# Decoding chosen expert pairs through two one-hot rows of 16, and giving all weight splits of routing to GpSimd

## The chip, the cores and the metric

The kernel runs on one core of one Trainium2 chip. The metric is the device time of one execution in microseconds; the median of the runs is given. In the profile PE is TensorE, DVE VectorE, ACT ScalarE, POOL GpSimd and SP SyncE, which issues the loads.

## The reference

Two layers of a network for 512 tokens with 1024 features. The first is a layer with sparse attention and a state-space branch; the second has a band attention, a gated delta rule and, at its end, `peer`, in which the change lies. `peer` takes 128 tokens at a time:

```python
qry = rms_norm_2((hb @ w_query).reshape(128, 8, 256), query_gain)
s1 = einsum("thd,nd->thn", qry[..., :128], sub_keys_1)      # 128 keys
s2 = einsum("thd,nd->thn", qry[..., 128:], sub_keys_2)      # 128 keys
v1, i1 = top_k(s1, 16)
v2, i2 = top_k(s2, 16)
cand_s = (v1[..., :, None] + v2[..., None, :])              # 16 x 16 pairs
cand_i = (i1[..., :, None] * 128 + i2[..., None, :])
top_s, pos = top_k(cand_s, 16)
experts = take_along_axis(cand_i, pos, axis=-1)
gates = softmax(top_s)
u, vv = expert_down[experts], expert_up[experts]
act = gelu(einsum("thkd,td->thk", u, hb))
out = einsum("thk,thkd->td", gates * act, vv)
```

So each token and each of 8 heads picks 16 of 16384 experts: for each chosen pair the position among the candidates has to be turned into the two key numbers.

## The kernel before, in words

Instructions are recorded in Python order and a scheduler then sets a fixed order for each engine; an engine works through its own queue in that order and waits at its head. A matrix product is done with operands split in two parts, high and low, in three passes (`mm3`, L71 to L74). Weights are loaded by SP into `wr`, ScalarE makes the high part `wh` (L51), and `wl`, the low part, is a subtraction on VectorE or GpSimd (L52), 128 x 1024 elements; the parameter `eng` says which.

`peer` has these stages. `routing` makes the 16 query projections and then, for token blocks 3, 0, 1, 2 of 128 tokens, the choice of experts. Tokens of blocks 0, 1 and 2 go through all experts densely: `down` is one projection of 384 tokens on 128 experts with a GELU, `g_build` makes the weights of the experts, `up_block` and `up_mm` multiply by the second matrix. Tokens of block 3 take their experts' rows by indirect DMA, issued on GpSimd (`gather_steps`), and multiply them on VectorE (L1667, L1680). `fill(x, eng)` puts x `down` projections at the place where it is called, as work for TensorE; its `eng` goes to the split of the weights. `gstep(n)` puts n gather steps there.

In `routing`, `best(t)` makes the scores of two heads at a time on TensorE (L1405), ScalarE copies them to `sc` (L1406), and VectorE finds the 16 best of 128 keys with MAX8, FIND_INDEX8 and MATCH_REPLACE8 (L1410 to L1414). `choose(t)` then forms 50 candidate sums `cand` for each of 8 heads (of 16 x 16 pairs only those with (a + 1)(b + 1) up to 16 can be chosen), finds the 16 best and their positions `pf`, and decodes the positions. `code` holds 128 i1 + i2 of the 50 candidates, built on GpSimd in `codef`. For two heads at a time VectorE compares `pf` with `iota50` into `eq` (L1459), 50 rows of 16, GpSimd multiplies `eq` by `code` as 32-bit words (L1463), and six additions on VectorE sum the 50 rows (L1465), cast to `ex` (L1466). `route_end` makes the softmax of the 16 sums; for block 3 it casts `ex` to `idx`, the gather's list; for the others it takes `ex` apart into the two keys by a shift and a mask (L1511 to L1517), transposes them on TensorE and leaves 16-bit lists for `g_build`.

`choose` of one block and `best` of the next are generators that alternate: after each `yield` of `choose`, `best` does two heads. Block 3's `best` runs alone first.

Of the kernel before, what the change touches and what calls it, by code (L numbers as in the profile page):

```python
# [20 lines left out]
P = 128  # L21
# [5 lines left out]
class Kernel:  # L27
# [1318 lines left out]
    def routing(self, rt):  # L1346
        nc, I, pp, pr = self.nc, self.i, self.pp, self.pr
        V, G = nc.vector, nc.gpsimd
# [3 lines left out]
        for j in range(2):  # L1352
            k = self.load(rt, f"peer_k{j}", [P, P])
            V.tensor_scalar(k, k, qg[:, j:j + 1], None, op0=OP.mult)
            keys.append(k)
        iota50 = self.t(rt, [P, 50, 16], F16, "iota50")
        G.iota(iota50, [[1, 50], [0, 16]], base=0, channel_multiplier=0, allow_small_or_imprecise_dtypes=True)
        sel = self.t(rt, [P, 8, 8], F32, "sel")
        G.affine_select(sel, self.ones[:, :64].rearrange("p (a b) -> p a b", a=8), [[1, 8], [-1, 8]],
                        OP.is_equal, 0.0, base=0, channel_multiplier=0)  # L1360
# [15 lines left out]
        p = self.t(pr, [P, T], F32, "a", 5)  # L1376
# [16 lines left out]
        def best(t, out):  # L1393

            tt = slice(t * P, t * P + P)
            vv = self.t(rt, [P, 8, 2, 16], F32, "vv", 2)
            ii = self.t(rt, [P, 8, 2, 16], U32, "ii", 2)
            out += [vv, ii]
            for hp in range(4):
                ps = self.t(pr, [P, T], F32, "a", 5).rearrange("p (a n) -> p a n", a=4)  # L1400
                s = self.t(rt, [P, 4, P], F32, "sc", 2)
                for j in range(2):
                    h = 2 * hp + j
                    for k in range(2):
# [12 lines left out]
                self.fill(1.25, G if hp % 2 else None)  # L1417
                yield

        def choose(t, vv, ii):  # L1420

            fi = self.t(rt, [P, 8, 2, 16], F32, "fi", 1)
            V.tensor_copy(fi, ii)
            V.tensor_scalar(fi[:, :, 0], fi[:, :, 0], 128.0, None, op0=OP.mult)

            cand = self.t(rt, [P, 8, 50], F32, "cand", 1)
            code = self.t(rt, [P, 8, 50], I32, "code", 1)
            codef = self.t(rt, [P, 8, 50], F32, "codef", 1)
            off = 0
            for a in range(9):  # L1430
                n = 16 // (a + 1) if a < 8 else 8
                o = slice(off, off + n)
                for eng, dst, src in ((V, cand, vv), (G, codef, fi)):
                    if a < 8:
                        eng.tensor_add(dst[:, :, o], src[:, :, 1, :n], src[:, :, 0, a:a + 1].to_broadcast([P, 8, n]))  # L1435
                    else:
                        eng.tensor_add(dst[:, :, o], src[:, :, 0, 8:16], src[:, :, 1, 0:1].to_broadcast([P, 8, n]))
# [12 lines left out]
            pf = self.t(rt, [P, 8, 16], F16, "pf", 1)  # L1450
            V.tensor_copy(pf, pi_)
            yield
            ex = self.t(rt, [P, 8, 16], F32, "ex", 1)
            for h in range(0, 8, 2):

                sh = [P, 2, 50, 16]
                hh = slice(h, h + 2)
                eq = self.t(rt, sh, I16, "eq", 3)
                V.tensor_tensor(eq, pf[:, hh].unsqueeze(2).to_broadcast(sh), iota50[:, None].to_broadcast(sh),  # L1459
                                op=OP.is_equal)  # L1460

                e2 = eq.bitcast(I32)
                G.tensor_mul(e2, e2, code[:, hh].unsqueeze(3).to_broadcast([P, 2, 50, 8]))  # L1463
                for m, n in ((25, 25), (13, 12), (7, 6), (4, 3), (2, 2), (1, 1)):
                    self.pace = V.tensor_tensor(eq[:, :, :n], eq[:, :, :n], eq[:, :, m:m + n], op=OP.add)  # L1465
                V.tensor_copy(ex[:, hh], eq[:, :, 0])  # L1466
                if t != 3:
                    self.gstep(1)
                self.fill(1, G)
                if h == 2:  # L1470
                    yield
            self.fill(2, G)
            self.route_end(rt, t, ts, ex)
# [16 lines left out]

    def route_end(self, rt, t, ts, ex):

        nc, pp, pr = self.nc, self.pp, self.pr
        V = nc.vector
        sh = [P, 8, 16]
        e = self.t(rt, sh, F32, "ge", 1)
        V.tensor_sub(e, ts, ts[:, :, 0:1].to_broadcast(sh))
        nc.scalar.activation(e, e, AF.Exp)
        sm = self.t(rt, [P, 8], F32, "gs", 1)
        V.tensor_reduce(sm, e, axis=AX.X, op=OP.add)  # L1500
        V.reciprocal(sm, sm)
        fl = "p h k -> p (h k)"
        if t == 3:
# [280 lines left out]
```

## Time and profile before

| | us |
|---|---|
| median of 3 runs | 2604.02 |
| lowest and highest run | 2603.02, 2606.86 |
| the profiled execution | 2602.06 |
| its span, first to last instruction | 2600.3 |
| TensorE, VectorE, ScalarE, GpSimd busy | 2458.6, 1889.7, 1052.5, 709.0 |

Busy time is the time in which an engine had at least one instruction running. In the rows below, a line number is a line of the kernel before; `out<-in` are tiles by the program's names; after a bar come busy time and the mean duration of one, then the idle time of the engine just ahead of those instructions and what ended it.

### The profile page before, as it was taken

Reading aid. Unit: us, or ns where it says so; the run is one execution under the profiler, and the core shown is the slowest. Engines: PE = TensorE matmul, PEld = TensorE weight load, DVE = VectorE, ACT = ScalarE, POOL = GpSimd, SP = SyncE. Lnnn points to the kernel's source line nnn. Section 1 sums busy time; section 2 is a strip of 40 time slices with the busy share of each in tenths; the row PEclk is TensorE's granted clock in tenths of the full one; section 3 lists DMA queues with packets and bytes.
Section 4 is the critical chain, followed back from the end, with each engine's and each line's share of the span. In section 5 each row is a group of like instructions: output and inputs, shape, how many; then the busy total and the mean of one; then the engine's idle time right before and its main releaser. Section 6 shows DMA issues by size and latency. Waiting matters only on the chain. (4 is left out here: it accounts for less than half of the span.)

```text
span 2600.3 us, 34898 instructions
## 1 busy us (share of the span) xinstructions
PE 2458.6 (95%) x12577; PEld 2051.7 (79%) x12577; DVE 1889.7 (73%) x3704; ACT 1052.5 (40%) x1881; POOL 709.0 (27%) x554
## 2 busy tenths in 40 slices
PE   5999999999999999899998887999989999999999
PEld 4777777768788779776778887899978888888887
DVE  8795666667764773565428899998767788888877
ACT  4444466653322444344433333354433333333332
POOL 3240011010001122511104566321344343443431
PEclk9999999999999999999999988999999999999999
DMA  7222212228865311111322455698999999989995
GB/s 243 77 81 83 72 65 65 74 75 298 283 225 172 98 57 49 49 37 57 128 81 82 149 175 160 230 328 319 338 333 319 336 337 343 352 305 334 341 333 211
DMA packets 199597, 500.44 MB, mean 192 GB/s; under 512 B 20096, under 2 KB 85888, under 8 KB 196352
## 3 DMA queue, kind: packets, MB, share of 16 engines
q1 hardware_dynamic: 159104, 338.81, 39.2%
q0 software_dynamic: 36864, 134.23, 14.6%
q10 hardware_dynamic: 3456, 25.17, 2.4%
q8 instruction: 99, 1.62, 0.3%
q14 instruction: 74, 0.61, 0.1%
HBM read 448.01 MB, written 50.14 MB: 192 GB/s over the span
## 5 line engine op out<-in xcount | busy, mean ns | idle before, releaser
L74 PE MATMUL g<-hh,wl 128*128 128x384 f32 (+1 forms) x1792 | 663.6, 370 | 42.0 <-DVE wl L52 23.2
L51 ACT ACTIVATE wh<-wr 128x1024 fp32r<-128x1024 f32 (+2 forms) x424 | 442.7, 1046 | 630.8 <-PE g L73 345.8
L72 PE MATMUL g<-hh,wh 128*128 128x384 f32 (+1 forms) x1792 | 668.3, 373 | 9.4 <-ACT act L1624 7.8
L73 PE MATMUL g<-hl,wh 128*128 128x384 f32 (+1 forms) x1792 | 660.4, 369 | 0.0
L52 DVE TENSOR_TENSOR wl<-wr,wh 128x1024 fp32r<-128x1024 f32 (+3 forms) x370 | 453.7, 1227 | 210.8 <-ACT wh L51 208.6
L74 PEld LDWEIGHTS g<-hh,wl 128*128 128x128 f32 x1792 | 344.5, 192 | 81.2 <-DVE wl L52 24.8
L72 PEld LDWEIGHTS g<-hh,wh 128*128 128x128 f32 x1792 | 344.5, 192 | 44.3 <-ACT act L1624 8.7
L73 PEld LDWEIGHTS g<-hl,wh 128*128 128x128 f32 x1792 | 344.1, 192 | 40.6 <-issue 10.3
L73 PE MATMUL acc<-wl,gh 128*128 128x512 f32 x768 | 303.8, 396 | 0.0
L74 PE MATMUL acc<-wh,gl 128*128 128x512 f32 x768 | 303.7, 395 | 0.0
L72 PE MATMUL acc<-wh,gh 128*128 128x512 f32 x768 | 303.7, 395 | 0.0
L1661 POOL DMA_INDIRECT row<-in_rows_dn,idx x128 | 162.9, 1273 | 342.2 <-DVE row L1667 289.9
L1661 POOL DMA_INDIRECT row<-in_rows_up,idx x128 | 173.1, 1352 | 271.5 <-DVE gacc L1680 250.8
L51 ACT ACTIVATE gh<-ga 128x384 fp32r<-128x384 f32 x128 | 67.2, 525 | 336.1 <-issue 196.4
L52 POOL TENSOR_TENSOR wl<-wr,wh 128x1024 fp32r<-128x1024 f32 x54 | 132.7, 2463 | 214.0 <-ACT wh L51 204.2
L1667 DVE SCALAR_TENSOR_TENSOR row<-row,h2n 128x1024 f32<-128x1024 f32 x128 | 160.6, 1261 | 23.1 <-DMA row<-in_rows_dn,idx 23.0
L1680 DVE SCALAR_TENSOR_TENSOR gacc<-row,gw,gacc 128x1024 f32<-128x1024 f32 x127 | 162.5, 1280 | 12.9 <-DMA row<-in_rows_up,idx 12.2
L74 PEld LDWEIGHTS acc<-wh,gl 128*128 128x128 f32 x768 | 144.4, 188 | 34.7
L73 PEld LDWEIGHTS acc<-wl,gh 128*128 128x128 f32 x768 | 144.4, 188 | 34.4
L72 PEld LDWEIGHTS acc<-wh,gh 128*128 128x128 f32 x768 | 144.4, 188 | 34.4
L52 DVE TENSOR_TENSOR gl<-ga,gh 128x384 fp32r<-128x384 f32 x128 | 73.2, 572 | 58.0 <-ACT gh L51 58.0
L98 PE MATMUL g<-wh,hh 128*128 128x512 f32 (+3 forms) x256 | 96.1, 377 | 13.4 <-ACT hh L223 11.8
(551 smaller groups left out, 3919.8 us busy)
## 6 DMA issues: line engine op xcount, KB each, us to landing
wr<-in_w_dn SPq DMA_DIRECT2D x128, 512.0 KB, 4.7
wr<-in_w_up SPq DMA_DIRECT2D x128, 512.0 KB, 6.8
wr<-in_ada_w SPq DMA_DIRECT2D x56, 512.0 KB, 4.6
g_d<-stage ACTq DMA_DIRECT2D x24, 1024.0 KB, 9.0
gr<-g_d SPq DMA_DIRECT2D x32, 768.0 KB, 9.6
wr<-in_w_x SPq DMA_DIRECT2D x24, 512.0 KB, 3.4
act_d<-act SPq DMA_DIRECT2D x63, 192.0 KB, 4.8
ar<-act_d SPq DMA_DIRECT2D x63, 192.0 KB, 6.1
```

The source lines that it names most:

```text
L51: nc.scalar.activation(hi, src, AF.Copy)
L52: eng.tensor_sub(lo, src, hi.bitcast(F32))
L72: mm(ps, ah, bh, start=first, stop=False)
L73: mm(ps, ah, bl, start=False, stop=False)
L74: self.mm = mm(ps, al, bh, start=False, stop=last)
L98: mm(pss[t], hh[:, tt], wh[:, k], start=f, stop=False)
L1661: nc.gpsimd.indirect_dma_start(r, None, src, bass.IndirectOffsetOnAxis(ap=self.idx[:, s:s + 1], axis=0))
L1667: nc.vector.scalar_tensor_tensor(r, r, 1.0, self.h2n, op0=OP.mult, op1=OP.mult, accum_out=act[:, s:s + 1])
L1680: nc.vector.scalar_tensor_tensor(acc, r, w[:, s:s + 1], acc, op0=OP.mult, op1=OP.add)
```

## The change

The position of a chosen candidate is no longer looked up in a list of 50 codes. The candidates lie in rows: row a of the first eight has 16 // (a + 1) entries, so a comparison with the start of each next row (`first`) counts the row number, and a product with the row lengths (`count`) sums up where the row starts. That gives, for each of 128 chosen positions, the two ranks a and b below 16. The last 8 positions are the ranks 8 to 15 of the first key with rank 0 of the second, added by `px`. Then one comparison with `iota16` makes one-hot rows of 16 for all heads and both keys, 4096 f16 elements; they are multiplied by the key numbers `iif` and summed in four halvings to the two keys `f1`. All of it is on VectorE. `codef`, `code`, the multiplication on GpSimd, and the taking apart in `route_end` go; for block 3, 128 times the first key plus the second is formed in `route_end`. The fills of routing all give GpSimd as the engine of their splits, two of them at another place in `choose`; the gather steps stand in pairs.

```diff
-        iota50 = self.t(rt, [P, 50, 16], F16, "iota50")
-        G.iota(iota50, [[1, 50], [0, 16]], base=0, channel_multiplier=0, allow_small_or_imprecise_dtypes=True)
+        iota16 = self.t(rt, [P, 16, 16], F16, "iota16")
+        G.iota(iota16, [[1, 16], [0, 16]], base=0, channel_multiplier=0, allow_small_or_imprecise_dtypes=True)
+        first = self.t(rt, [P, 8, P], F16, "first")
+        count = self.t(rt, [P, 8, P], F16, "count")
...
+            G.memset(first[:, j], float(off))
+            G.memset(count[:, j], float(n))
...
-                self.fill(1.25, G if hp % 2 else None)
+                self.fill(1.25, G)
...
-            fi = self.t(rt, [P, 8, 2, 16], F32, "fi", 1)
-            V.tensor_copy(fi, ii)
-            V.tensor_scalar(fi[:, :, 0], fi[:, :, 0], 128.0, None, op0=OP.mult)
+            iif = self.t(rt, [P, 256, 2], F16, "iif", 1)
+            V.tensor_copy(iif, ii.rearrange("p h k n -> p (h k n)").unsqueeze(2).to_broadcast([P, 256, 2]))
...
-                for eng, dst, src in ((V, cand, vv), (G, codef, fi)):
...
-            G.tensor_copy(code, codef)
...
+            V.tensor_copy(pf, pi_.rearrange("p h k -> p (h k)"))
+            self.fill(2, G)
             yield
-            ex = self.t(rt, [P, 8, 16], F32, "ex", 1)
-            for h in range(0, 8, 2):
...
-                V.tensor_tensor(eq, pf[:, hh].unsqueeze(2).to_broadcast(sh), iota50[:, None].to_broadcast(sh),
-                                op=OP.is_equal)
-                e2 = eq.bitcast(I32)
-                G.tensor_mul(e2, e2, code[:, hh].unsqueeze(3).to_broadcast([P, 2, 50, 8]))
-                for m, n in ((25, 25), (13, 12), (7, 6), (4, 3), (2, 2), (1, 1)):
-                    self.pace = V.tensor_tensor(eq[:, :, :n], eq[:, :, :n], eq[:, :, m:m + n], op=OP.add)
-                V.tensor_copy(ex[:, hh], eq[:, :, 0])
-                if t != 3:
-                    self.gstep(1)
-                self.fill(1, G)
...
+            sh = [P, 8, P]
+            ge = self.t(rt, [P, 2, 8, P], F16, "ge2", 1)
+            V.tensor_tensor(ge[:, 0], pf[:, None, :].to_broadcast(sh), first, op=OP.is_ge)
+            V.tensor_tensor(ge[:, 1], ge[:, 0], count, op=OP.mult)
+            for m in (4, 2, 1):
+                V.tensor_tensor(ge[:, :, :m], ge[:, :, :m], ge[:, :, m:2 * m], op=OP.add)
...
+            V.tensor_scalar(x, pf, -42.0, 0.0, op0=OP.add, op1=OP.max)
+            V.tensor_tensor(ge[:, 0, 0], ge[:, 0, 0], x, op=OP.add)
+            V.tensor_tensor(ge[:, 1, 0], ge[:, 1, 0], x, op=OP.add)
+            hk = "p (h k) -> p h k"
+            V.tensor_copy(ab[:, :, 0], ge[:, 0, 0].rearrange(hk, h=8))
+            V.tensor_tensor(ab[:, :, 1], pf.rearrange(hk, h=8), ge[:, 1, 0].rearrange(hk, h=8), op=OP.subtract)
+            sh = [P, 16, 16, 16]
+            eq = self.t(rt, sh, F16, "eq", 1)
+            self.pace = V.tensor_tensor(eq, ab.rearrange("p h k n -> p (h k) n").unsqueeze(2).to_broadcast(sh),
+                                        iota16[:, None].to_broadcast(sh), op=OP.is_equal)
+            if t != 3:
+                self.gstep(2)
             self.fill(2, G)
+            yield
+            e4 = eq.rearrange("p q c (s two) -> p (q c) s two", two=2)
+            V.tensor_tensor(e4, e4, iif.unsqueeze(2).to_broadcast([P, 256, 8, 2]), op=OP.mult)
+            for m in (8, 4, 2):
+                V.tensor_tensor(eq[:, :, :m], eq[:, :, :m], eq[:, :, m:2 * m], op=OP.add)
...
+            for k in range(2):
+                self.pace = V.tensor_tensor(f1[:, k].rearrange(hk, h=8), e5[:, :, k, 0], e5[:, :, k, 1], op=OP.add)
+            if t != 3:
+                self.gstep(2)
+            self.fill(2, G)
+            self.route_end(rt, t, ts, f1)
...
+            V.scalar_tensor_tensor(f1[:, 0], f1[:, 0], 128.0, f1[:, 1], op0=OP.mult, op1=OP.add)
+            V.tensor_copy(self.idx, f1[:, 0])
...
-        V.tensor_scalar(c1, ci, 7, None, op0=OP.arith_shift_right)
-        V.tensor_scalar(ci, ci, 127, None, op0=OP.bitwise_and)
```

VectorE, the decoding of block 3 (the first one), before. `vv`, `ii` and `sc` belong to `best` of block 0, `wl` is the split of a filler's weights; a number at a name's end tells buffers apart.

```order
L1412 MATCH_REPLACE sc_11855<-vv_11748,sc_11855 128x128
L1459 TENSOR_TENSOR eq_11915<-pf_11852,iota_2588_10817 128x1600
L1413 MAX vv_11748<-sc_11855 128x8
L1459 TENSOR_TENSOR eq_11957<-pf_11852,iota_2588_10817 128x1600
L1414 MAX_INDEX ii_11749<-vv_11748,sc_11855 128x8
L1465 TENSOR_TENSOR eq_11915<-eq_11915 128x2x400
L52 TENSOR_TENSOR wl_12030<-wr_12028,wh_12029 128x1024
L1465 TENSOR_TENSOR eq_11915<-eq_11915 128x2x192
L1465 TENSOR_TENSOR eq_11957<-eq_11957 128x2x400
```

The same place after.

```order
L1465 TENSOR_TENSOR ge_2766_11983<-ge_2766_11983 128x2x128
L1527 TENSOR_TENSOR gate_g_12201<-ge_12195,gs_12198 128x128
L1470 TENSOR_TENSOR ge_2766_11983<-ge_2766_11983,px_11990 128x128
L1471 TENSOR_TENSOR ge_2766_11983<-ge_2766_11983,px_11990 128x128
L1473 COPY ab_11989<-ge_2766_11983 128x8x16
L1474 TENSOR_TENSOR ab_11989<-pf_11857,ge_2766_11983 128x8x16
L1478 TENSOR_TENSOR eq_11996<-ab_11989,iota_2588_10817 128x4096
L1485 TENSOR_TENSOR eq_11996<-eq_11996,iif_11741 128x4096
L1419 MAX vv_11753<-sc_11924 128x8 x2
```

The decoding stands in one piece where it was mixed with rounds of `best`, and no split of a filler's weights stands in it.

GpSimd, from the middle of the first decoding to the first gathers, before.

```order
L1463 TENSOR_TENSOR eq_11957<-eq_11957,code_11727 128x800
L52 TENSOR_TENSOR wl_12072<-wr_12070,wh_12071 128x1024
L1463 TENSOR_TENSOR eq_12059<-eq_12059,code_11727 128x800
L52 TENSOR_TENSOR wl_12114<-wr_12112,wh_12113 128x1024
L1463 TENSOR_TENSOR eq_12101<-eq_12101,code_11727 128x800
L52 TENSOR_TENSOR wl_12146<-wr_12144,wh_12145 128x1024
L1661 DMA row_12398<-in_rows_dn,idx_12217 128x1024
L52 TENSOR_TENSOR wl_12179<-wr_12177,wh_12178 128x1024
```

The same place after; `row` is the destination of a gather.

```order
L52 TENSOR_TENSOR wl_12033<-wr_12031,wh_12032 128x1024
L52 TENSOR_TENSOR wl_12093<-wr_12091,wh_12092 128x1024
L52 TENSOR_TENSOR wl_12132<-wr_12130,wh_12131 128x1024
L1676 DMA row_12372<-in_rows_dn,idx_12203 128x1024
L1676 DMA row_12549<-in_rows_dn,idx_12203 128x1024
L1676 DMA row_12601<-in_rows_dn,idx_12203 128x1024
L52 TENSOR_TENSOR wl_12165<-wr_12163,wh_12164 128x1024
L1676 DMA row_12604<-in_rows_dn,idx_12203 128x1024
```

Splits follow one another without multiplications between them, and three gathers stand ahead of the next split where one stood.

TensorE, the first scores of block 0, before. `a` with three numbers are the scores of three pairs of heads, `g` is a filler's product.

```order
L1405 MATMUL a_11750<-c_peer_k_10814,qT_2601_10888 128x128
L72 MATMUL g_11778<-hh_2524_10637,wh_11780 128x384
L73 MATMUL g_11778<-hl_2525_10638,wh_11780 128x384
L1405 MATMUL a_11854<-c_peer_k_10811,qT_2619_10997 128x128
L1405 MATMUL a_11854<-c_peer_k_10814,qT_2625_11032 128x128
L1405 MATMUL a_11999<-c_peer_k_10811,qT_2643_11141 128x128
L74 MATMUL g_11778<-hh_2524_10637,wl_11781 128x384
```

The same place after.

```order
L1414 MATMUL a_11755<-c_peer_k_10814,qT_2603_10906 128x128
L72 MATMUL g_11783<-hh_2524_10637,wh_11785 128x384
L73 MATMUL g_11783<-hl_2525_10638,wh_11785 128x384
L74 MATMUL g_11783<-hh_2524_10637,wl_11786 128x384
L72 MATMUL g_11783<-hh_2526_10639,wh_11785 128x384
L73 MATMUL g_11783<-hl_2527_10640,wh_11785 128x384
```

The scores of the second and third pair no longer begin inside the first pair's filler; they stand behind later fillers.

## Rows read from the trace of the kernel before

**Rows 1.** The page's head: the span; busy us, share of the span, instructions

```profile
span 2600.3 us, 34898 instructions
...
PE 2458.6 (95%) x12577; PEld 2051.7 (79%) x12577; DVE 1889.7 (73%) x3704; ACT 1052.5 (40%) x1881; POOL 709.0 (27%) x554
```

**Rows 2.** Five stretches of routing: busy us and instructions of each engine, clock, DMA

```profile
1379.60:1398.40 18.80, 18.05 (x112) 17.53 (x113) 18.74 (x129) 8.15 (x15) 4.24 (x2) 1.00 0.18 58
1398.40:1457.60 59.20, 50.76 (x277) 49.65 (x277) 48.91 (x245) 21.22 (x33) 37.42 (x28) 0.91 0.40 128
1457.60:1530.40 72.80, 60.18 (x315) 58.67 (x315) 68.70 (x269) 23.68 (x37) 39.98 (x31) 0.86 0.54 175
1530.40:1608.90 78.50, 59.07 (x317) 57.38 (x316) 75.00 (x273) 22.87 (x38) 47.22 (x34) 0.87 0.52 158
1608.90:1646.60 37.70, 28.97 (x145) 27.70 (x143) 36.05 (x124) 11.66 (x16) 26.11 (x23) 0.91 0.50 151
sum 267.00, PE 217.04 PEld 210.92 DVE 247.40 ACT 87.58 POOL 154.96; mean PE 43.41 PEld 42.18 DVE 49.48 ACT 17.52 POOL 30.99
```

**Rows 3.** Groups from 1379 to 1650 us: busy us, mean ns, idle before

```profile
L52 POOL TENSOR_TENSOR wl<-wr,wh 128x1024 fp32r<-128x1024 f32 x35 | 85.4, 2447 | 32.0 <-ACT wh L51 30.8 <-DVE ts L1448 1.0
...
L1465 DVE TENSOR_TENSOR eq<-eq 128x64 int16<-128x64 int16 (+5 forms) x96 | 56.5, 628 | 5.6 <-POOL eq L1463 5.4
...
L1463 POOL TENSOR_TENSOR eq<-eq,code 128x800 int32<-128x800 int32 x16 | 31.7, 1993 | 29.8 <-DVE eq L1459 14.5 <-DVE eq L1465 7.0 <-issue 6.9
L1661 POOL DMA_INDIRECT row<-in_rows_dn,idx x24 | 27.1, 1129 | 35.8 <-DVE eq L1465 14.7 <-DVE ex L1466 6.0 <-DVE idx L1507 5.8
...
L1459 DVE TENSOR_TENSOR eq<-pf,iota 128x1600 int16<-128x1600 f16 x16 | 15.6, 981 | 0.0
...
L52 DVE TENSOR_TENSOR wl<-wr,wh 128x1024 fp32r<-128x1024 f32 x9 | 14.5, 1617 | 11.3 <-ACT wh L51 11.3
L1514 DVE TENSOR_SCALAR ci<-ci 128x128 int32<-128x128 int32 x3 | 11.0, 3674 | 0.1
...
L1466 DVE CAST ex<-eq 128x32 f32<-128x32 int16 x16 | 9.6, 603 | 0.0
```

**Rows 4.** The tile `eq`: duration in ns, shortest, median, longest

```profile
L1465 DVE TENSOR_TENSOR eq<-eq x96: 156/246/4543, 1420.3 to 1643.0; 128x800 int16<-128x800 int16 x16, 128x384 int16<-128x384 int16 x16, 128x192 int16<-128x192 int16 x16, 128x96 int16<-128x96 int16 x16
```

**Rows 5.** Timeline of VectorE and GpSimd, 1398 to 1460 us

```profile
1398.37 0.28 DVE L1435 TENSOR_TENSOR cand<-vv 128x128 f32<-128x128 f32 x1
1398.56 0.29 DVE L1423 CAST fi<-ii 128x256 f32<-128x256 uint32 x1
...
1452.58 2.69 POOL L52 TENSOR_TENSOR wl<-wr,wh 128x1024 fp32r<-128x1024 f32 x1
...
1452.92 0.48 DVE L1410 MAX8 vv<-sc 128x8 f32<-128x128 f32 x2
...
1457.09 2.40 POOL L52 TENSOR_TENSOR wl<-wr,wh 128x1024 fp32r<-128x1024 f32 x1 [1.83 <-ACT wh L51]
...
1457.61 2.03 DVE L1435 TENSOR_TENSOR cand<-vv 128x128 f32<-128x128 f32 x1
```

**Rows 6.** Timeline of VectorE at the last query projection

```profile
1368.24 1.23 DVE L52 TENSOR_TENSOR wl<-wr,wh 128x1024 fp32r<-128x1024 f32 x1 [10.32 <-ACT wh L51]
1369.38 0.68 DVE L1370 TENSOR_TENSOR psq<-psq,psq 128x512 f32<-128x512 f32 x1
```

**Rows 7.** Timeline of VectorE in the last route_end

```profile
1645.48 0.22 DVE L1511 CAST ci<-ex 128x128 int32<-128x128 f32 x1
1645.73 0.23 DVE L1513 TENSOR_SCALAR c<-ci 128x128 int32<-128x128 int32 x1
```

**Rows 8.** Groups by shape, VectorE, 1650 to 1900 us (g_build)

```profile
L1580 DVE TENSOR_TENSOR ob<-i,io 128x1024 f16<-128x1024 f16 x48 | 32.9, 685 | 4.6 <-PE a L1591 4.5
```

**Rows 9.** Timeline of ScalarE, two fillers in a row

```profile
1547.75 1.06 ACT L51 ACTIVATE wh<-wr 128x1024 fp32r<-128x1024 f32 x1 [2.72 <-issue]
...
1551.91 1.06 ACT L51 ACTIVATE wh<-wr 128x1024 fp32r<-128x1024 f32 x1 [2.72 <-issue]
```

More of the change, by code (lines that the diff above doesn't have):

```diff
@@ L1355, in routing @@
             keys.append(k)
-        iota50 = self.t(rt, [P, 50, 16], F16, "iota50")
-        G.iota(iota50, [[1, 50], [0, 16]], base=0, channel_multiplier=0, allow_small_or_imprecise_dtypes=True)
+        iota16 = self.t(rt, [P, 16, 16], F16, "iota16")
+        G.iota(iota16, [[1, 16], [0, 16]], base=0, channel_multiplier=0, allow_small_or_imprecise_dtypes=True)
+        first = self.t(rt, [P, 8, P], F16, "first")
+        count = self.t(rt, [P, 8, P], F16, "count")
+        off = 0
+        for j in range(8):
+            n = 16 // (j + 1)
+            off += n
+            G.memset(first[:, j], float(off))
+            G.memset(count[:, j], float(n))
         sel = self.t(rt, [P, 8, 8], F32, "sel")
@@ L1416, in best @@
                     self.gstep(1)
-                self.fill(1.25, G if hp % 2 else None)
+                self.fill(1.25, G)
                 yield
         def choose(t, vv, ii):
-            fi = self.t(rt, [P, 8, 2, 16], F32, "fi", 1)
-            V.tensor_copy(fi, ii)
-            V.tensor_scalar(fi[:, :, 0], fi[:, :, 0], 128.0, None, op0=OP.mult)
+            iif = self.t(rt, [P, 256, 2], F16, "iif", 1)
+            V.tensor_copy(iif, ii.rearrange("p h k n -> p (h k n)").unsqueeze(2).to_broadcast([P, 256, 2]))
             cand = self.t(rt, [P, 8, 50], F32, "cand", 1)
-            code = self.t(rt, [P, 8, 50], I32, "code", 1)
-            codef = self.t(rt, [P, 8, 50], F32, "codef", 1)
             off = 0
@@ L1432, in choose @@
                 o = slice(off, off + n)
-                for eng, dst, src in ((V, cand, vv), (G, codef, fi)):
[L1434 to L1437, printed above, removed]
+                if a < 8:
+                    V.tensor_add(cand[:, :, o], vv[:, :, 1, :n], vv[:, :, 0, a:a + 1].to_broadcast([P, 8, n]))
+                else:
+                    V.tensor_add(cand[:, :, o], vv[:, :, 0, 8:16], vv[:, :, 1, 0:1].to_broadcast([P, 8, n]))
                 off += n
-            G.tensor_copy(code, codef)
             yield
@@ L1449, in choose @@
                 V.max_index(pi_[:, h, 8:16], ts[:, h, 8:16], c)
-            pf = self.t(rt, [P, 8, 16], F16, "pf", 1)
-            V.tensor_copy(pf, pi_)
+            pf = self.t(rt, [P, P], F16, "pf", 1)
+            V.tensor_copy(pf, pi_.rearrange("p h k -> p (h k)"))
+            self.fill(2, G)
             yield
-            ex = self.t(rt, [P, 8, 16], F32, "ex", 1)
-            for h in range(0, 8, 2):
-                sh = [P, 2, 50, 16]
-                hh = slice(h, h + 2)
-                eq = self.t(rt, sh, I16, "eq", 3)
-                V.tensor_tensor(eq, pf[:, hh].unsqueeze(2).to_broadcast(sh), iota50[:, None].to_broadcast(sh),
-                                op=OP.is_equal)
-                e2 = eq.bitcast(I32)
-                G.tensor_mul(e2, e2, code[:, hh].unsqueeze(3).to_broadcast([P, 2, 50, 8]))
-                for m, n in ((25, 25), (13, 12), (7, 6), (4, 3), (2, 2), (1, 1)):
-                    self.pace = V.tensor_tensor(eq[:, :, :n], eq[:, :, :n], eq[:, :, m:m + n], op=OP.add)
-                V.tensor_copy(ex[:, hh], eq[:, :, 0])
-                if t != 3:
-                    self.gstep(1)
-                self.fill(1, G)
-                if h == 2:
-                    yield
@@ L1472, in choose @@
-            self.fill(2, G)
-            self.route_end(rt, t, ts, ex)
+            sh = [P, 8, P]
[4 more added lines that the diff above has]
+                V.tensor_tensor(ge[:, :, :m], ge[:, :, :m], ge[:, :, m:2 * m], op=OP.add)
+            ab = self.t(rt, [P, 8, 2, 16], F16, "ab", 1)
@@ new lines, in choose @@
+            x = self.t(rt, [P, P], F16, "px", 1)
+            V.tensor_scalar(x, pf, -42.0, 0.0, op0=OP.add, op1=OP.max)
[5 more added lines that the diff above has]
+            sh = [P, 16, 16, 16]
@@ new lines, in choose @@
+            for m in (8, 4, 2):
+                V.tensor_tensor(eq[:, :, :m], eq[:, :, :m], eq[:, :, m:2 * m], op=OP.add)
+            f1 = self.t(rt, [P, 2, P], F32, "f1", 1)
+            e5 = eq.rearrange("p (h k) c s -> p h k c s", k=2)
+            for k in range(2):
[4 more added lines that the diff above has]
+            self.route_end(rt, t, ts, f1)
@@ L1489, in routing, with route_end @@
                 self.rows(rt)
-    def route_end(self, rt, t, ts, ex):
+    def route_end(self, rt, t, ts, f1):
         nc, pp, pr = self.nc, self.pp, self.pr
@@ L1506, in route_end @@
             self.idx = self.t(pp, [P, P], U32, "idx")
-            V.tensor_copy(self.idx, ex.rearrange(fl))
+            V.scalar_tensor_tensor(f1[:, 0], f1[:, 0], 128.0, f1[:, 1], op0=OP.mult, op1=OP.add)
+            V.tensor_copy(self.idx, f1[:, 0])
             return
         V.tensor_mul(e, e, sm.unsqueeze(2).to_broadcast(sh))
-        ci = self.t(rt, [P, P], I32, "ci", 1)
-        V.tensor_copy(ci, ex.rearrange(fl))
-        c1 = self.t(rt, [P, P], I32, "c1", 1)
-        V.tensor_scalar(c1, ci, 7, None, op0=OP.arith_shift_right)
-        V.tensor_scalar(ci, ci, 127, None, op0=OP.bitwise_and)
-        f1 = self.t(rt, [P, 2, P], F32, "f1", 1)
-        V.tensor_copy(f1[:, 0], c1)
-        V.tensor_copy(f1[:, 1], ci)
         p = self.t(pr, [P, T], F32, "a", 5)
```

## The prediction

> **What bounds the kernel now.** I read the page's head first: TensorE is busy 95% of a 2600.3 us span [rows 1], so time can only come out of stretches where TensorE is not full. I then cut routing into its five steps by the times at which `cand` starts [rows 2]: best(3) alone, then choose of block 3, 0, 1 and 2, each beside best of the next block. There VectorE is the fullest engine, 247.4 us of 267.0, against 217.0 for TensorE and 155.0 for GpSimd. Everything in this stage sits in fixed queues; what TensorE does in it is 44 projections of `down`, used as filler, plus the score products. A shorter VectorE queue lets the same filler run closer together, and the stages behind it do not change: by the code routing calls for 16 x 1.25 + 4 x 6 = 44 fills and 8 + 12 = 20 gather steps before as after. So I price VectorE's queue in this stage, and TensorE's 217.0 us is the floor: the stage cannot lose more than about 50 us.
>
> The groups in the stage [rows 3] show where VectorE's time goes: the 96 tree additions on `eq` take 0.628 us on average, but their median is 0.246 us and their longest 4.543 us [rows 4]. The same for the mask of `ci`: 3.674 us for 128 elements. The timeline shows why [rows 5]: `cand`, two inputs from SBUF, takes 0.28 us with GpSimd idle; at 1457.61 it takes 2.03 us and ends just after the GpSimd split that began at 1457.09 and lasted 2.40. MAX8, with one input, starts at 1452.92 inside another split and is not stretched. So a split on GpSimd holds up a two-input VectorE instruction until it is through.
>
> The Trainium skill, "SBUF — State Buffer", section Who interferes with whom, says so as a rule: a VectorE instruction with two SBUF inputs contends with a GpSimd instruction that reads SBUF, and the loser blocks for the whole instruction. This speaks against the change, since 44 splits of 2.4 us now all lie on GpSimd; taken strictly it makes the first rival below the forecast, about 2614 us, where the rows, with less than half of GpSimd's time felt, give about 2585.
>
> **What goes.** From [rows 3]: 96 additions at 0.628 are 60.3 us, 16 compares at 0.981 are 15.7, 16 casts to `ex` 9.6, three masks 11.0. Of VectorE's nine splits in the stretch three belong to the next stage (they stand in both orders); the six others go to GpSimd: 14.5 less 3 x 1.23 [rows 6] is 10.8. That is 107.4 us in 137 instructions. An instruction starts about 0.09 us before the end of the one ahead of it when it needn't wait for it (1398.37 + 0.28 against 1398.56 [rows 5]), so 137 x 0.08 or 11 us of that is overlap: 96. In route_end four more small ones go in each of three blocks, 0.25 us from start to start [rows 7]: 3. Together 99 us. The cast to `iif` replaces the one to `fi`; I set them equal.
>
> **What comes.** No decoding instruction of the new kind is in the trace, so I draw a line through two 16-bit rows: 1600 elements in 0.981 us [rows 3] and 1024 in 0.685 [rows 8], so 0.159 us plus 0.514 ns an element. Per block: three passes over 1024 elements (compare, product, first addition), 0.685 each; additions of 512 and 256, 0.42 and 0.29; five of 128 (px, two additions, copy, subtraction), 0.22 each; compare and product over 4096, 2.26 each; additions of 2048, 1024 and 512, 1.21, 0.69 and 0.42; two of 128 to f32, 0.28 each as `cand`. Sum: 2.06 + 0.71 + 1.10 + 4.52 + 2.32 + 0.56 = 11.3 us in 17 instructions. Nearly each needs the one ahead; such a pair has 0.03 us between end and start (1645.48 + 0.22 against 1645.73 [rows 7]), so 11.8 us, and 47 us for four blocks.
>
> Their waits for GpSimd are the unknown. By the line the 96 additions would take 28.2 us unheld (0.57, 0.36, 0.26, 0.21, 0.19, 0.18 for the six sizes, 16 times); they take 60.3, so 32 us are waits. The casts hold 16 x (0.603 - 0.22) or 6, the masks 3 x (3.674 - 0.23) or 10. That is 48 us in 115 instructions, 0.42 each: 68 new ones would wait 28 us. Counted the other way, 48 us are 41% of what GpSimd spent on splits and code multiplications (85.4 + 31.7); afterwards it has 44 splits, 108 us, and 41% of that is 44 us. I take the middle, 36. The ends: nothing, and 24 splits that stand in choose, each holding one decoding instruction for its full 2.45 us, 59 us.
>
> **The rest.** The moved splits cost GpSimd 2.45 us where VectorE took 1.23; there are eight (six here, two ahead of the stretch), 20 us; but 16 code multiplications (31.7 us) and the additions to `codef` leave it, so it ends with 108 us of splits and 20 gathers of 1.13 us, 23 us, in a stage of some 240: hidden. If the cover were gone, the split would be late for the third product of its projection, and TensorE would wait up to 2.4 us. VectorE sat idle 11.3 us ahead of splits of its own, waiting for ScalarE [rows 3]; those waits go, but TensorE was behind there too, so I count 5 of the 11 (ends 0 and 11). TensorE runs a filler every 4.16 us [rows 9], so 14 of them, 58 us from 1379.6, still gate the last scores of block 0. Ahead of routing two splits move from VectorE to GpSimd while the last queries are squared: `psq` then starts behind a split of 2.45 us instead of 1.23 [rows 6], 1.2 us later, and TensorE waits for it, twice: 2.5 us lost. The sixteen fills of `first` and `count` stand on GpSimd before `sel`, in a stretch where GpSimd has nothing else: 0.
>
> **Sum.** 99 - 47 - 36 + 5 - 2.5 = 18.5 us, say 19. The profiled execution took 2602.06 us around its span of 2600.3, and the median of the runs is 2604.02. From the median: 2585 us. With no waits the sum is 54 and TensorE's floor cuts it to 48: 2556. With all of them and no idle time won back it is -9.5.
>
> **Rivals.**
> Every split in choose holds a decoding instruction to the full. For it: the new decode is 17 instructions almost in one piece, nearly all with two SBUF inputs, where the old one had MAX8 rounds between its head pairs. Against it: 59% of GpSimd's time was not felt so far, and the long compares were held little (981 ns on average over 16 [rows 3]). Price 59 us in place of 36, no idle won back: 2604 + 9.5, 2614. It turns slower than before once the waits pass 49 us, 20 of the 24 splits.
>
> TensorE or GpSimd becomes the pace and eats the gain. For it: the scores of the second and third head pair stand one to three fillers later in TensorE's order than before, and on GpSimd each split now stands behind the gathers, which wait for VectorE to free a row. If each of the eight moved splits comes its 2.45 us late, TensorE stands, and VectorE stands for the scores behind it, 20 us go: 2605, no change. Against: GpSimd itself stood 32.0 us ahead of its splits for ScalarE's `wh` [rows 3], so it was the early one of the two, and in all steps but the second VectorE has clearly more to do than TensorE [rows 2].
>
> The 16-bit passes run at half rate because of their repeated operands. Each element would cost 0.514 ns more; 15,600 elements a block are 8 us, 32 for four, so 2617. Against: the pass of [rows 8] repeats an operand in pairs just as the product with `iif` does, and is fast.
>
> The waits all but vanish, because TensorE spaces the splits out and most fall on MAX8 rounds: 2556.
>
> **Chances.** Forecast 0.66 (its own range 2568 to 2598), waits vanish 0.10, held to the full 0.12, pace 0.09, half rate 0.03. A measurement of this kernel tells about 0.2% from no change, 5.2 us; so faster 0.76, same 0.09, slower 0.15. The range 2556 to 2609 takes in the first, most of the pace case and the edge of the second; outside are the two slower cases and a little of the upside.
>
> **What would show it.** After: the stretch from the first MAX8 to the last f1 should take about 246 us (217 to 274); compare and product over 4096 elements at 2.3 us where unheld; one kind of GpSimd work beside 20 gathers, 44 splits at 2.45. Right if VectorE's decode rows sum to 75 to 95 us. Wrong if they pass 100 us, if VectorE shows new waits for scores from ScalarE, or if a 4096 pass takes 4.4 us unheld.

## The result, and the profile after

| | before | after |
|---|---|---|
| median us | 2603.52 (2601.19 to 2606.86) | 2574.10 (2573.65 to 2574.48) |
| span of the profiled execution | 2600.3 | 2572.8 |

Four runs each; the ratio is 0.9886, interval 0.9873 to 0.9898: 29.4 us faster. The forecast was 2585, so right in sign and range, and 11 us short. The page's head after, beside [rows 1]:

```profile
span 2572.8 us, 34773 instructions
...
PE 2451.5 (95%) x12577; PEld 2043.5 (79%) x12577; DVE 1867.7 (73%) x3618; ACT 1052.5 (41%) x1881; POOL 693.8 (27%) x522
```

I compare routing from the first MAX8 on `vv` to the first `ob` of the next stage, since the ends of `choose` differ between the two programs. The windows of before, then of after (PE, PEld, DVE, ACT, POOL busy, clock, DMA):

```profile
1379.66:1649.65 269.99, 220.05 (x1178) 213.97 (x1179) 250.38 (x1039) 89.11 (x138) 154.90 (x115) 0.89 0.48 149
```

```profile
1380.10:1620.07 239.97, 212.66 (x1178) 205.95 (x1179) 226.99 (x955) 88.78 (x138) 132.24 (x65) 0.94 0.54 167
```

The stretch lost 30.0 us: VectorE's busy time 23.4, its idle time 6.6. Around it the profile has three small sums. From the first `psq` to the first MAX8 it is 95.2 us before and 97.6 after, 2.4 lost, as forecast (2.5). From the last `ob` to the first product of the up stage it is 60.8 and 62.8, 2.0 lost, which nobody forecast. And the first `psq` came 2.0 earlier, ahead of all that the change touches; in the runs below it lies between 1281.9 and 1291.6 us, so single profiles differ by some us there, and I read stretches, not spans. (The 2.0 ahead of the up stage may be of that kind: there the other runs lie between 60.1 and 62.3.)

The groups of the stretch after, beside [rows 3, 4]:

```profile
L52 POOL TENSOR_TENSOR wl<-wr,wh 128x1024 fp32r<-128x1024 f32 x41 | 100.6, 2462 | 58.0 <-ACT wh L51 57.6
L1682 DVE SCALAR_TENSOR_TENSOR row<-row,h2n 128x1024 f32<-128x1024 f32 x20 | 31.0, 1571 | 0.0
L1487 DVE TENSOR_TENSOR eq<-eq 128x2048 f16<-128x2048 f16 (+2 forms) x12 | 17.6, 1465 | 0.4
L1419 DVE MAX8 vv<-sc 128x8 f32<-128x128 f32 x64 | 15.1, 277 | 11.6 <-ACT sc L1415 11.6
L1441 DVE TENSOR_TENSOR cand<-vv 128x16 f32<-128x16 f32 (+5 forms) x32 | 11.4, 422 | 0.0
L1485 DVE TENSOR_TENSOR eq<-eq,iif 128x4096 f16<-128x4096 f16 x4 | 11.3, 2836 | 0.0
L1478 DVE TENSOR_TENSOR eq<-ab,iota 128x4096 f16<-128x4096 f16 x4 | 9.2, 2292 | 0.1
...
L1470 DVE TENSOR_TENSOR ge<-ge,px 128x128 f16<-128x128 f16 x4 | 7.4, 1854 | 0.0
L1471 DVE TENSOR_TENSOR ge<-ge,px 128x128 f16<-128x128 f16 x4 | 5.3, 1322 | 0.0
...
L52 DVE TENSOR_TENSOR wl<-wr,wh 128x1024 fp32r<-128x1024 f32 x3 | 3.6, 1220 | 0.6 <-ACT wh L51 0.6
```

The comparison over 4096 takes the 2.3 us worked out; the product over 4096 takes 2.84 us on average, held in part. The short `ge` additions of 128 elements take 1.3 and 1.9 us on average. Where that comes from is in the timeline of VectorE and GpSimd in the first decoding (start, us):

```profile
1417.13 4.76 POOL L52 TENSOR_TENSOR wl<-wr,wh 128x1024 fp32r<-128x1024 f32 x2 [10.22 <-ACT wh L51]
...
1417.19 2.47 DVE L1527 TENSOR_TENSOR gate_g<-ge,gs 128x128 f32<-128x128 f32 x1
1419.59 2.39 DVE L1470 TENSOR_TENSOR ge<-ge,px 128x128 f16<-128x128 f16 x1
1421.90 0.21 DVE L1471 TENSOR_TENSOR ge<-ge,px 128x128 f16<-128x128 f16 x1
...
1422.41 2.29 DVE L1478 TENSOR_TENSOR eq<-ab,iota 128x4096 f16<-128x4096 f16 x1
```

Two splits back to back hold two instructions, one each; the next one, after 1421.89, is free. And the `L1419` row shows a wait that the prediction named as a sign against it: VectorE stood 11.6 us for scores. The same row of before:

```profile
L1410 DVE MAX8 vv<-sc 128x8 f32<-128x128 f32 x64 | 16.1, 278 | 4.1 <-ACT sc L1406 4.1
```

But this wait is not new. In both kernels 3.84 us of the row lie ahead of the first MAX8; what is added after is one stand of VectorE, ahead of the scores of block 0's last two heads, and the kernel before has it too; there one of VectorE's own splits is next in its queue, and the wait is listed with the split (before, then after):

```profile
1451.78 1.23 DVE L52 TENSOR_TENSOR wl<-wr,wh 128x1024 fp32r<-128x1024 f32 x1 [9.05 <-ACT wh L51]
```

```profile
1449.60 0.49 DVE L1419 MAX8 vv<-sc 128x8 f32<-128x128 f32 x2 [7.57 <-ACT sc L1415]
```

Without its split VectorE would have stood as long before: ScalarE's copy of these scores ended at 1452.50. So up to this place, some 70 us into the stretch, TensorE's row of fillers, in which these scores stand, sets the time at which routing goes on, with 8.4 us of waits of its own for low parts before and 2.05 after.

### The profile page after: what moved, and what is told of

Read it like the earlier page. It is cut to its first block, busy times and chain, and to the rows that moved or that the text cites. A ratio compares the mean times of both kernels' runs of the same rounds, so it can differ in the third digit from the quotient of the medians.

```text
span 2572.8 us, 34773 instructions
## 1 busy us (share of the span) xinstructions
PE 2451.5 (95%) x12577; PEld 2043.5 (79%) x12577; DVE 1867.7 (73%) x3618; ACT 1052.5 (41%) x1881; POOL 693.8 (27%) x522
## 5 line engine op out<-in xcount | busy, mean ns | idle before, releaser
L52 DVE TENSOR_TENSOR wl<-wr,wh 128x1024 fp32r<-128x1024 f32 (+3 forms) x362 | 440.4, 1217 | 189.7 <-ACT wh L51 187.3
L72 PEld LDWEIGHTS g<-hh,wh 128*128 128x128 f32 x1792 | 342.4, 191 | 52.8 <-ACT act L1639 10.8
L52 POOL TENSOR_TENSOR wl<-wr,wh 128x1024 fp32r<-128x1024 f32 x62 | 152.5, 2468 | 239.5 <-ACT wh L51 230.6
L1682 DVE SCALAR_TENSOR_TENSOR row<-row,h2n 128x1024 f32<-128x1024 f32 x128 | 166.3, 1309 | 21.7 <-DMA row<-in_rows_dn,idx 21.7
L1695 DVE SCALAR_TENSOR_TENSOR gacc<-row,gw,gacc 128x1024 f32<-128x1024 f32 x127 | 162.6, 1280 | 11.8 <-DMA row<-in_rows_up,idx 10.8
```

What stands on the lines that cost most here:

```text
L52: eng.tensor_sub(lo, src, hi.bitcast(F32))
L72: mm(ps, ah, bh, start=first, stop=False)
L1682: nc.vector.scalar_tensor_tensor(r, r, 1.0, self.h2n, op0=OP.mult, op1=OP.mult, accum_out=act[:, s:s + 1])
L1695: nc.vector.scalar_tensor_tensor(acc, r, w[:, s:s + 1], acc, op0=OP.mult, op1=OP.add)
```

## The experiments

Theory A: VectorE's queue sets the pace of routing; the new decoding is the gain; a GpSimd split costs VectorE what it holds up. Rivals: B, the move of the splits is the gain; C, TensorE's fillers set the pace now; D, the long VectorE instructions hide TensorE's wait for the low part; G, the fillers' new places are the gain.

All times in us; each ratio is to runs of the kernel before taken with that version (medians 2602.1 to 2603.7). Stretch as above, from one profiled execution each; the columns behind it are VectorE in the stretch, busy times summed over the groups of a kind (all rows that write `eq`, `ge` from `pf` or in f16, `px`, `ab`, `iif` or `fi`, `f`, `ex`, `ci`, `c` are decoding; gathers are the products of L1682 with their accumulator reads; softmax is `ge` in f32, `gs`, `gate_g`, `gT`, `gl`, `pf`, `idx`, `gw`; own splits are the `wl` that VectorE makes; idle is the stretch less VectorE's busy time).

| kernel | median | ratio, interval | stretch | decoding | gathers | softmax | `cand` | own splits | idle |
|---|---|---|---|---|---|---|---|---|---|
| before | 2603.5 | | 270.0 | 103.1 | 27.0 | 7.5 | 13.0 | 14.5 | 19.6 |
| after | 2574.1 | 0.9873 to 0.9898 | 240.0 | 70.5 | 32.6 | 14.2 | 13.8 | 3.6 | 13.0 |
| old engines | 2572.4 | 0.9867 to 0.9900 | 239.1 | 71.1 | 29.3 | 13.7 | 11.6 | 12.6 | 9.3 |
| decoding alone | 2574.8 | 0.9872 to 0.9905 | 242.7 | 66.2 | 33.7 | 12.5 | 13.6 | 14.9 | 10.8 |
| old decoding, all on GpSimd | 2609.8 | 1.0010 to 1.0029 | 273.4 | 114.1 | 27.5 | 9.9 | 11.1 | 3.6 | 21.5 |
| comparison twice | 2585.0 | 0.9911 to 0.9944 | 248.4 | 84.2 | 30.6 | 14.9 | 13.8 | 3.6 | 8.9 |
| no splits in choose | 2542.0 | 0.9747 to 0.9779 | 205.9 | 47.1 | 28.0 | 7.2 | 6.7 | 2.4 | 22.1 |
| split unused | 2572.6 | 0.9864 to 0.9897 | 235.6 | 77.5 | 31.2 | 8.4 | 16.2 | 2.4 | 7.4 |
| choose on VectorE | 2568.3 | 0.9849 to 0.9882 | 232.3 | 56.3 | 25.3 | 9.3 | 6.7 | 34.3 | 12.0 |
| all on VectorE | 2567.7 | 0.9851 to 0.9884 | 233.9 | 46.1 | 25.4 | 7.0 | 6.5 | 52.2 | 9.3 |
| fillers into best | 2571.9 | 0.9863 to 0.9898 | 236.8 | 71.1 | 34.5 | 11.6 | 13.8 | 3.6 | 9.9 |
| halves | 2570.8 | 0.9848 to 0.9899 | 241.1 | 70.0 | 33.7 | 14.9 | 16.5 | 3.5 | 10.1 |
| quarters | 2568.4 | 0.9846 to 0.9881 | 233.1 | 68.9 | 31.9 | 10.3 | 14.9 | 3.5 | 11.0 |
| VectorE and quarters | 2566.7 | 0.9845 to 0.9877 | 233.6 | 52.7 | 26.4 | 8.9 | 6.9 | 34.0 | 15.1 |

### Which part is the gain

**Old engines** in `best`:

```diff
-                self.fill(1.25, G)
+                self.fill(1.25, G if hp % 2 else None)
```

> The new decoding, but with the old division of the splits in best: 8 of the 44 go back to VectorE. Theory A (VectorE's queue sets the pace of routing, a GpSimd split costs VectorE only what it holds up): 6 of them lie in the stretch, 6 x 1.23 = 7 us more on VectorE, up to 5 us of new idle time for ScalarE's high part, less some holds: 2574 + 8, 2582 us (2577 to 2587). Theory B (moving the splits brought most of the gain): 2574 + 20 or more, 2594 us or above. Theory C (TensorE's row of fillers sets the pace now): within 3 us of 2574.

2572.4: not 8 us slower but the same, outside A's range and where C put it; C is taken up by the comparison twice. **Decoding alone**, with the fillers' old places too:

```diff
-                self.fill(1.25, G)
+                self.fill(1.25, G if hp % 2 else None)
...
             V.tensor_copy(pf, pi_.rearrange("p h k -> p (h k)"))
-            self.fill(2, G)
...
-            self.fill(2, G)
+            self.fill(4, G)
             self.route_end(rt, t, ts, f1)
```

> The new decoding with the old division of the splits in best, and with the fillers of choose standing late as before (none after the positions, two after the comparison, four at the end): nothing but the decoding is changed, but for gather steps in pairs. Theory A (the decoding brings the gain, places and engines of the fillers little): 2572 us as with the old engines, within 4. Rival G (the gain needs the fillers' new places, which keep TensorE fed while VectorE decodes): 2582 us or above.

2574.8: the whole gain is there with neither the engines nor the places of the fillers changed (the gather steps stay in pairs); B and G fall. How much of it is the shorter work on VectorE, and how much the multiplication that GpSimd no longer has, no run separates. The other half by itself, **the old decoding with all splits on GpSimd** (in the kernel before):

```diff
-                self.fill(1.25, G if hp % 2 else None)
+                self.fill(1.25, G)
```

> The old decoding, but with all 44 splits of routing on GpSimd. Theory A: 7 us less on VectorE and 2 to 5 us of idle time, but GpSimd is fuller beside the old decoding and holds it up 0.4 x 2.45 = 1 us for each of 6 more splits: 2604 - 4, 2600 us (2594 to 2605). Theory B: most of the 29 us are already here, 2585 us or below.

6 us slower than before, where I expected 4 faster and A's range ended at 2605. Its profiled execution is the slowest of ten, 2615.7, with 7 us of that ahead of routing; its stretch is 3.4 us longer than before's:

```profile
L1465 DVE TENSOR_TENSOR eq<-eq 128x192 int16<-128x192 int16 (+5 forms) x96 | 62.0, 680 | 4.5 <-POOL eq L1463 4.2
...
L1410 DVE MAX8 vv<-sc 128x8 f32<-128x128 f32 x64 | 15.5, 277 | 16.7 <-ACT sc L1406 16.6
```

The additions of [rows 3] are held longer (680 ns against 628). In the table 10.9 us of own splits go, 11.0 us of decoding and 2.4 of softmax come, and 1.9 of idle time; with the 2.4 us ahead of the stretch the move costs more than it saves. The 16.7 us in the row of scores, in place of 4.1, are again the stand at block 0's last scores, here 11.03 us. The scores are not late in this run: they are copied 71.8 us after the first MAX8, before 72.4; VectorE comes sooner and stands. With old engines and the new decoding the row reads 4.0, because a split of VectorE's own has the wait, 5.73 us:

```profile
L1419 DVE MAX8 vv<-sc 128x8 f32<-128x128 f32 x64 | 15.4, 278 | 4.0 <-ACT sc L1415 4.0
```

```profile
1446.81 2.98 DVE L52 TENSOR_TENSOR wl<-wr,wh 128x1024 fp32r<-128x1024 f32 x1 [5.73 <-ACT wh L51]
```

There the scores are copied at 65.6 us, after the change at 69.0; ahead of the latter a filler waited 2.05 us for its low part from GpSimd.

### Is VectorE the pace, and is it GpSimd that holds it

**The comparison twice** (the statement at L1478 repeated):

> The changed kernel with the comparison of 4096 elements issued twice in each block, 4 x 2.29 = 9.2 us more of VectorE and nothing else. Theory A: 2574 + 9, 2583 us (2579 to 2587). Theory C: the added work lies beside fillers, 2577 us or below.

10.9 us slower for 9.2 us of work, the stretch 8.4: C falls for the stretch as a whole. It holds up to the stand: the repeated comparison of block 3 shortens that from 7.57 to 5.12 us. The decoding grows by 13.7 us, 4.5 more than the work, and idle time shrinks by 4.1, so the near equality is partly chance. **No splits in choose:**

```diff
+            if eng == "skip":
+                return
...
-            self.fill(2, G)
+            self.fill(2, "skip")
...
+        if eng == "skip":
+            wl = wh
```

> The changed kernel without the splits of the 24 fillers in choose: their third product takes the high part of the weights again, so the low part of these weights is left out of the result. Theory A (a split on GpSimd holds two-input instructions of VectorE): the 23 us of holds on the decoding and some 10 us on the gathers' products and the softmax go, less what falls to TensorE's 213 us: 2574 - 25, 2549 us (2542 to 2558). Rival D (the long durations of these instructions do not come from GpSimd's splits, or hide behind TensorE): 2568 us or above.

**Split unused:** the same, but the split is made on GpSimd and nobody reads it:

```diff
-            self.fill(2, G)
+            self.fill(2, "unused")
...
-        wh, wl = self.wload(self.i["w_dn"][b], eng)
+        wh, wl = self.wload(self.i["w_dn"][b], self.nc.gpsimd if eng == "unused" else eng)
+        if eng == "unused":
+            wl = wh
```

> The 24 splits in choose are still done on GpSimd, but the third product reads the high part, so that TensorE does not wait for them and the low part of these weights is left out of the result. Without the splits the kernel took 2542 us. Theory A (VectorE is held up by GpSimd's work): the 32 us stay: 2574 us, within 5. Theory D (TensorE's wait for the low part): 2542 us, within 5. Between them, the two share the 32 us.

2542.0 and 2572.6. With TensorE's wait gone and the splits kept, 1.5 of the 32 us come back; with the splits gone, all. D falls. The windows, no splits first:

```profile
1381.94:1587.84 205.90, 198.69 (x1172) 193.74 (x1173) 183.80 (x955) 88.81 (x138) 72.37 (x41) 1.00 0.61 194
```

```profile
1383.02:1618.63 235.61, 209.61 (x1174) 205.01 (x1175) 228.26 (x955) 88.92 (x138) 133.86 (x65) 0.94 0.54 167
```

Same instructions on VectorE, 955, and 44.5 us less busy. **Choose on VectorE** (`self.fill(2, None)` in `choose`) and **all on VectorE** (in `best` too) take the holds away without leaving work out:

> The changed kernel with the 24 splits of the fillers in choose on VectorE. It has 24 x 1.23 = 29.5 us more to do; taking these splits away altogether was worth 32 us. Theory A (what a GpSimd split costs is the hold on VectorE): the holds of 32 us go, 29.5 us of splits and some idle time for ScalarE's high part come: 2574 + 3, 2577 us (2570 to 2586). Theory D (the 32 us were TensorE's wait for GpSimd): VectorE's 29.5 us are added to nothing won but that wait: 2574 as well if the wait goes entirely, and then TensorE's idle time for the low part, not VectorE's long instructions, is what has gone in the trace; 2595 us or above if it stays.

> All 44 splits of routing on VectorE, nothing of them on GpSimd. Against the version with those of choose on VectorE (2568 us): 18 more splits in the stretch, 18 x 1.23 = 22 us; the holds that remain there, some 11 us on the decoding and 2 elsewhere, go; 2.4 us come back ahead of the stretch, where the squares of the queries stood behind GpSimd's splits. Theory A: 2568 + 22 - 13 - 2, 2575 us (2569 to 2583). If a split beside MAX8 rounds were no cheaper on GpSimd than on VectorE: 2566 us or below.

2568.3 (2566.2 to 2570.9) and 2567.7 (2566.0 to 2570.0): both lie 5 to 6 us under the change (2573.7 to 2574.5), and both below A's range. The ratios' intervals overlap with the change's; the runs do not. With the splits of `choose` moved, 33.5 us of holds went (decoding 14.2, gathers 7.3, softmax 4.9, `cand` 7.1) and 30.7 us of splits came, near A's 32 and 29.5; the new idle time that A added did not come (12.0 against 13.0). These rows give 3.8 of the 7.6 us by which the stretch is shorter; the rest is overlap between neighbouring instructions, which the sums by group do not show. With the splits of `best` moved as well the time stays the same: 2567.7 lies between A's range and the last case of the second expectation, nearer to the latter, so these splits are hardly cheaper on GpSimd than on VectorE. Groups of the second, beside those of after:

```profile
L52 DVE TENSOR_TENSOR wl<-wr,wh 128x1024 fp32r<-128x1024 f32 x43 | 52.2, 1216 | 8.8 <-ACT wh L51 8.7
L1682 DVE SCALAR_TENSOR_TENSOR row<-row,h2n 128x1024 f32<-128x1024 f32 x20 | 23.8, 1211 | 0.0
...
L1487 DVE TENSOR_TENSOR eq<-eq 128x2048 f16<-128x2048 f16 (+2 forms) x12 | 9.2, 766 | 0.0
L1478 DVE TENSOR_TENSOR eq<-ab,iota 128x4096 f16<-128x4096 f16 x4 | 9.1, 2277 | 0.0
L1485 DVE TENSOR_TENSOR eq<-eq,iif 128x4096 f16<-128x4096 f16 x4 | 9.1, 2274 | 0.0
...
L1471 DVE TENSOR_TENSOR ge<-ge,px 128x128 f16<-128x128 f16 x4 | 0.9, 215 | 0.0
L1470 DVE TENSOR_TENSOR ge<-ge,px 128x128 f16<-128x128 f16 x4 | 0.8, 212 | 0.0
```

This is the unheld price of every row, and the difference to after is what GpSimd's splits hold: decoding 70.5 - 46.1 = 24.4, gathers 7.2, softmax 7.2, `cand` 7.3, together 46 us for 41 splits of 100.6 us: 1.12 us of VectorE a split, where VectorE does it itself in 1.21. That the exchange is nearly even fits old engines and decoding alone, which came out like the change.

### Can the holds be made smaller

**Fillers into best:** `choose` keeps its fillers only in the last block.

```diff
-                self.fill(1.25, G)
+                self.fill(1.25 if t == 3 else 2.75, G)
...
-            self.fill(2, G)
+            self.fill(2 if t == 2 else 0, G)
```

> The changed kernel with the 18 fillers of choose of blocks 3, 0 and 1 moved into best beside them (2.75 at each of 12 places where 1.25 stood), the splits on GpSimd. Theory A: most of these splits lie beside MAX8 rounds, which are not held: two thirds of the 32 us x 18 / 24 come back, less new idle time for scores, which stand behind more fillers: 2574 - 10, 2564 us (2556 to 2576). Rival E (the scores stand behind too many fillers, and VectorE idles for them): 2580 us or above.

2571.9: inside A's range, but not by A's reason, and hardly apart from the change. E falls: the scores are not late (7.5 us of idle time ahead of the top-16 rounds, 11.7 after the change). But the decoding is held just as long, 71.1: the place of the call in the code did not keep splits out of it. What fits is that a split runs when ScalarE's high part is there, which ends 57.6 of the 58.0 us that GpSimd stood ahead of splits after the change; no run tried it by itself. **Halves and quarters:** each split as 2 or 4 instructions of GpSimd.

```diff
+            if isinstance(eng, int):
+                w = src.shape[1] // eng
+                for q in range(0, src.shape[1], w):
+                    nc.gpsimd.tensor_sub(lo[:, q:q + w], src[:, q:q + w], hi[:, q:q + w].bitcast(F32))
```

> The changed kernel with each of the 44 GpSimd splits of routing issued as two instructions of 512 elements. Theory A in its strict form (a VectorE instruction waits until the GpSimd instruction is through, and then has its turn): a hold lasts at most 1.2 us, and the second half waits for VectorE: about half of the holds of 23 + 12 us go: 2574 - 12, 2562 us (2555 to 2570). Theory F (the two share the port and VectorE merely runs slower beside GpSimd, so the work in all counts): no change, 2574 us within 4.

> The same in four instructions of 256 elements. Strict theory A: holds of at most 0.6 us each, three quarters of 35 us gone, less what the fixed cost of four GpSimd instructions and the waits of the splits behind VectorE give back: 2574 - 15, 2559 us (2548 to 2570). Theory F: 2574 us or a little above.

2570.8 (2566.2 to 2577.9, too wide to tell) and 2568.4 (2565.4 to 2571.5). The second lies at the upper end of A's range and under F's 2574, but A's reason fails: the decoding is held just as long (70.0 and 68.9). The halves in the same place as the timeline of after show why; four halves of GpSimd stand beside four instructions of VectorE:

```profile
1414.28 5.05 POOL L55 TENSOR_TENSOR wl<-wr,wh 128x512 fp32r<-128x512 f32 x4 [9.89 <-ACT wh L51]
...
1414.34 1.37 DVE L1532 TENSOR_TENSOR gate_g<-ge,gs 128x128 f32<-128x128 f32 x1
1415.64 1.29 DVE L1475 TENSOR_TENSOR ge<-ge,px 128x128 f16<-128x128 f16 x1
1416.85 1.31 DVE L1476 TENSOR_TENSOR ge<-ge,px 128x128 f16<-128x128 f16 x1
1418.09 1.29 DVE L1478 COPY ab<-ge 128x128 f16<-128x128 f16 x1
1419.30 0.21 DVE L1479 TENSOR_TENSOR ab<-pf,ge 128x128 f16<-128x128 f16 x1
```

Four instructions wait 1.1 us each where two waited 2.2: here the engines take turns, and smaller pieces make more, shorter holds. What the quarters win (5.7 us, the stretch 6.9) lies in other rows, softmax and idle, and I have no cause for it that a run singled out. **VectorE for choose, quarters for best:**

> The splits of choose on VectorE, those of best on GpSimd in four instructions of 256 elements. The two steps by themselves gave 2568 us each. Theory A: only 20 splits still hold anything up, some 13 us in all, of which finer turns save at most a third: 2568 - 3, 2565 us (2560 to 2572).

2566.7, inside A's range and 7 us below the change: its slowest run, 2568.4, is under the change's fastest, 2573.7. It beats both kernels, but can't be told from the two with the splits on VectorE, which are simpler.

## Why the prediction was right, and where it was short

**The signs.** The stretch, 240.0 us, lies where the prediction put it (217 to 274). The decoding rows sum to 70.5 us, under the 75 to 95 that were to show it right, and the row of scores rose from 4.1 to 11.6, a sign set against it; that one is the stand of before in another row.

**The bound.** Right but for the first 70 us: behind the stand VectorE's queue sets the pace; up to it the fillers ahead of block 0's last scores do, which the prediction names (14 of them). And TensorE's 217 us was no floor. Without splits in choose the stretch took 205.9 us, with the same fillers in 198.7 us of TensorE, busy 96% of it, at a granted clock of 1.00 (2.4 GHz throughout); before, it was busy 220.1 us, 82% of the stretch, and the clock was 0.89 (part of it at 1.2 GHz); 220.1 times 0.89 is 196. The same work measured at the lower clock was taken for a floor.

**What comes, unheld.** Right: 68 instructions were put at 45.2 us; all on VectorE shows 46.1 less 2.0 for `iif` and the product of block 3, 44.1. The half rate falls.

**The waits.** The mis-sized term. 36 us were to fall on the decoding; 24.4 did. The count of GpSimd's time felt, 41%, was near (46%), but I put all of it on the decoding. Of the 46.1 us of holds after, 21.7 fall on other work, where the prediction had nothing new: gathers' products 1.6 before and 7.2 after, softmax 0.5 and 7.2, `cand` 6.5 and 7.3 (each less its row of all on VectorE), 13.1 more. Together 37.5 against 36: the sum held, its place did not, and that is luck. The first rival, every split of choose felt whole, 59 us, is out, and so are vanishing waits.

**What goes, and the idle time.** The gap to the measured 30.0 us in the stretch (forecast 99 - 47 - 36 + 5 = 21) is made of small terms: 2.9 us less for the new instructions and their gaps, 2.5 because the cast to `iif` replaced 4.2 us of `fi` by 1.7 and not by the same, 2.7 in the rounds of the top 16 and 1.0 in the rest, 1.6 more idle time won, less 1.5 of waits: 9.2 for 9.0. The 2.7 is overlap: the durations of these rounds sum to 143.7 us in both kernels, but more of them stand back to back after. The idle time won is another than the one counted: 5.4 us before the additions, for GpSimd's product [rows 3], went, and I had not listed them; of the 11.3 us ahead of VectorE's own splits, of which I counted 5 as won, 9.05 are the stand, and 7.57 of that stayed, so 3.2 were won (11.3 less 0.6 that is left and 7.5 more ahead of scores).

**The moved splits.** Counted by themselves they were to bring about 7 us (10.8 and 5, less 2.5 and some 6 of holds). They brought nothing with the new decoding (2572.4 and 2574.8 without, 2574.1 with) and cost 6 us with the old. This step failed, and the decoding alone is worth 27 to 31 us, not 11. That the two errors have opposite signs brought the forecast nearer than its account deserves. The 2.5 us ahead of routing were right.

## What to carry to other kernels

Price a two-input instruction that moves to GpSimd by what it holds on VectorE, over all the work that lies beside it and not only the rows being changed; here 2.46 us of GpSimd cost VectorE 1.12, and VectorE did the same in 1.21, so the move was worth nothing. Fewer instructions on the engine that sets the pace are worth their time, and a version without the contending engine is the quickest way to read every unheld price at once. Look at where an engine stands, and not only at the row that has the wait: one stand can pass from row to row between two kernels.

## What the runs showed of the hardware

GpSimd waits as well: a split that starts inside a product of VectorE takes 3.12 us in place of 2.4 (after):

```profile
1470.64 1.21 DVE L1682 SCALAR_TENSOR_TENSOR row<-row,h2n 128x1024 f32<-128x1024 f32 x1
```

```profile
1470.98 3.12 POOL L52 TENSOR_TENSOR wl<-wr,wh 128x1024 fp32r<-128x1024 f32 x1 [10.32 <-ACT wh L51]
```

Instructions with one input were held too, so the two inputs of which the prediction speaks are not the whole condition: the masks of [rows 3] take 3.67 us on average for 128 elements. The Trainium skill, "SBUF — State Buffer", section Who interferes with whom, says that whichever issues first has the shared port for its whole instruction and that copies can be held too; both are seen here (the COPY of 1.29 us above, 0.18 unheld). A gather issued on GpSimd held no product that I could see: with all splits on VectorE and the gathers left, the products take 1211 ns on average, and the six of 20 that ran beside such an issue 1.21 to 1.22 us. That is shown for the products alone: a mask of before that had only such an issue beside it took 0.43 us, where [rows 7] have 0.23.
